# A hybrid decoder layer: T4 weight parts issued earlier in the mix stage, differences inside the attentions moved to VectorE, w_out's scaling spread

## The chip, the core and the metric

The kernel runs on one NeuronCore of a Trainium2 chip. The metric is the device time of one execution in microseconds (us). The engines are TensorE (PE, matmuls; PEld its weight loads), VectorE (DVE), ScalarE (ACT), GpSimd (POOL) and SyncE (SP), whose queue issues most of the transfers. TensorE writes its products to PSUM banks, ScalarE and VectorE read them there, GpSimd works on SBUF alone.

## What is computed

One layer with 2048 rows and a width of 1024, cut to its core:

```python
shift, scale, gate = split(silu(c) @ w_ada + b_ada)
u = x * (1 + scale) + shift
q, k, v, a_gate, p_in, p_gate, m_a, m_p = split(u @ w_in)
a = (sliding_window_sink_attention(q, k, v, sinks, bias) * silu(a_gate)) @ w_attn_proj
p = (group_linear(causal_pool(p_in)) * pool_scale * silu(p_gate)) @ w_pool_proj
y = ((sigmoid(m_a) * a + sigmoid(m_p) * p) @ w_out) * (1 + gate)
x = layer_norm(2 ** 0.25 * x + y) * ln_gain + ln_bias
```

All of it is in float32. Sixteen query heads share two heads of keys and values; the window is 128 rows.

## The kernel before

**Products by seven instead of eight.** Each large product is a Strassen-like scheme over 2 x 2 blocks. A weight block pair (a `Quad`) meets an input stored as seven sets, named B11, T1, T2, B21, T3, B22, T4: some are blocks of the input, some are differences of blocks. A product is made of 12 matmuls (`product`, line 314), because every float32 operand is split into a high and a low part: high times high (4 matmuls), high times low (4), low times high (4). The first eight need only the weights' high part, the last four the low part. The high part is a cast on ScalarE, the low part a subtraction on VectorE (`low`, line 131): `pair_split` (line 301) does two blocks at once, 128 x 1024, and `half_split` (line 307) one block, 128 x 512, for T4. Both write to `w_set` tiles, a ring of four buffers (line 167); a pair takes two, a half takes one.

**Rings.** Outside the attentions, `ring` (line 460) runs groups of two quads ("tiles"). For each group `back` (line 338) gives T2 and B21 of both tiles, then T3 and B22 of both, then T4 of both; `front` (line 328) then opens the next group with B11 and T1 of both. That is 14 products a group. T2, T3 and T4 of one tile add up in one bank `lg`; between T3 and T4 the sum `p5 = c + p5` (line 387) reads that bank. Each product is followed by `tick()`, which runs hooks: the loads, splits of sets, differences and stores that other stages hang into this group at a given position. `defer` puts work off by so many ticks, `q.consume` takes a finished result.

**Order.** Operations given through `act`, `dve`, `pool`, `pe` and `sp` (class `Ordered`, line 51) are pinned behind what was given out before them on their engine. Those given through `nc.scalar` and `nc.vector`, as in `back`, `pair_split` and `half_split`, can be moved by the framework's scheduler when they are ready sooner. Each engine then works its queue in order.

**Stages.** First ring (gates, keys, values, queries of the first half of the rows), attention of the first half, second ring, attention of the second half, then the mix stage: one leftover group, attention projection and pool projection of each half (two groups each, four phases), and the product with w_out. Only the quads of the four projection phases have gates to fetch (`ahead`). In the last group of a phase the hooks also split the sets of the next phase: `PLAN` and `SPLIT_AT` (lines 497 to 502) put them at ticks 2 to 7 and 11 to 13 of it, the rest into the next phase's first group. A set's half costs a ScalarE cast and a VectorE subtraction of 128 x 1024.

**Attentions.** `attention` (line 771) walks 64 blocks `n` of softmax work (scores, exponentials, transposes, values) and fills TensorE's time between them with products from `filling()`. `later(n, f)` runs `f` at the end of block `n`. All operations are pinned here. `sums_between` (line 996) hangs in, three times (at 39, 56 and 61), the differences T1, T2, T4 and T3 of the attention output that the mix stage will read: `sums_to` (line 199) loads two rooms of SBUF, makes four differences on GpSimd and stores them.

**w_out.** In the second ring, `second_phase` (line 1474) multiplies w_out by `cb` (1 + gate) on VectorE, row by row, before the same differences are made: the list `side`, hung in at the starts on line 1500; the last four starts are w_out's. In the first ring, `sums_to` does the same with x, modulated on ScalarE.

Of the kernel before, what the change touches and what calls it, by code (L numbers as in the profile page):

```python
# [60 lines left out]
def kernel(  # L61
# [134 lines left out]
    def put(q, store, name, i, src):  # L196
        q.dma_start(store[name][i // 2, :, i % 2, :], src)

    def sums_to(ph, store, i, load, work=None):

        b = []

        def x(r, c):
            return b[r][:, c * CH : (c + 1) * CH]

        def fetch():
            b.extend((ph.spare(), ph.spare()))
            b.reverse()
            for r in (1, 0):
                load(b[r], r)  # L210

        def sub(out, a, c):
            return lambda: pool.tensor_tensor(x(*out), x(*a), x(*c), ALU.subtract)

        todo = [(0, fetch)]
        if work:
            todo += [(4, lambda: work(b[0], 0)), (4.5, lambda: work(b[1], 1))]
        made = [("B11", (0, 0)), ("B21", (1, 0)), ("B22", (1, 1))] if work else []
        puts = [(5 + 0.6 * n, *x) for n, x in enumerate(made)]
        at = 7.5 if work else 4  # L220
        for out, a, c, name in (
            ((0, 1), (0, 1), (0, 0), "T1"),
            ((1, 1), (1, 1), (0, 1), "T2"),
            ((1, 0), (1, 0), (1, 1), "T4"),
            ((0, 0), (1, 1), (0, 0), "T3"),
        ):
            todo.append((at, sub(out, a, c)))
            puts.append((at + 2.5, name, out))
            at += 1.5
        for at, name, z in puts:  # L230
            todo.append((at, lambda name=name, z=z: put(sp, store, name, i, x(*z))))
        return sorted(todo, key=lambda t: t[0])
# [105 lines left out]
    def back(ph, grp, opened, nxt, own, tick):  # L338
        st = []
        for q in grp:  # L340
            if q.ahead:
                q.ahead(ph, 0)
                defer(2, lambda q=q: q.ahead(ph, 1))
        for q, (a, b, c, w, *copy) in zip(grp, opened):
            p5 = None if copy else ph.p("p5")
            if w is None:
                c = bank("lg")
                nc.scalar.copy(c, a)
                nc.scalar.copy(p5, b)
                w = pair_split(ph, q.second())[::-1]  # L350
                q.late()
                product(c, w[1], "T2")
            elif copy:
                p5 = copy[0]
            else:
                u2 = ph.p("u2")
                nc.scalar.copy(u2, a)
                if c is None:
                    c = bank("lg")
                    product(c, w[1], "T2", True)  # L360
                nc.vector.tensor_tensor(c, c, u2, ALU.add)
                nc.scalar.copy(p5, b)
            tick()
            if len(copy) < 2:
                nc.vector.tensor_tensor(b, c, p5, ALU.add)
            if not copy:
                product(a, w[0], "B21")
            tick()
            q.consume(ph, 0, 0, a)
            st.append((q, b, c, p5))  # L370
        w = {}

        def ask(q):

            defer(1, lambda: q.load(ph, own, nc.sync, None))
            defer(3, lambda: q.sum1(nc.gpsimd))

        def third(x):
            w[x] = opened[x][5] if len(opened[x]) > 5 else pair_split(ph, st[x][0].third())[::-1]
            if x < len(nxt):  # L380
                ask(nxt[x])

        def with_t3(x):
            q, b, c, p5 = st[x]
            product(c, w[x][1], "T3")
            tick()
            nc.vector.tensor_tensor(p5, c, p5, ALU.add)
            q.consume(ph, 1, 1, p5)

        def with_b22(x):  # L390
            q, b, c, p5 = st[x]
            product(b, w[x][0], "B22")
            tick()
            q.consume(ph, 0, 1, b)

        for x in range(len(st)):
            third(x)
            with_t3(x)
            with_b22(x)
        for q in nxt[len(st) :]:  # L400
            ask(q)
        for q, b, c, p5 in st:
            w = half_split(ph, q.a22)
            product(c, w, "T4")
            tick()
            q.consume(ph, 1, 0, c)

# [363 lines left out]
    def attention(ph, s, fills, post, opened):  # L771
# [18 lines left out]
        def later(n, f):  # L790
            coming.append((max(n, now_n[0]), len(coming), f))
# [202 lines left out]
            split(j)  # L994

        def sums_between(n0, i):
            for offset, f in [(0, rooms), *sums_to(ph, ain_d[s], i, load_raw(ain_d[s], i))]:
                later(n0 + int(offset / 2), f)

        def rooms():  # L1000
            ph.turns["spare"] = iter([kvp.tile([P, D], F32, tag=f"qs0{t}", name=f"room{t}") for t in range(2)])

        for i, n0 in enumerate((39, 56, 61)):
            sums_between(n0, i)
        fill = filling()
        lgs, exps, Ls, pvs, outs, ags = {}, {}, {}, {}, {}, {}
# [467 lines left out]
    def second_phase(ph, opened, post, plan1):  # L1474
        groups, fills, _, turn = plan1
        cb = ph.t.tile([P, D], F32, tag="cb", bufs=1, name="cb")
        hooks = {}

        def gate_rows():
            nc.scalar.dma_start(gate_d.rearrange("k p -> p k"), mod[:, 16:24], allow_slow_non_contiguous=True)  # L1480
            nc.scalar.dma_start(cb, gate_d.rearrange("k p -> (k p)").partition_broadcast(P))

        def load_wo(x, k):
            for n in range(2):
                sp.dma_start(cols(x, n), wout[k, n])

        side = []
        for raw, i in ((ain_d[0], 3), *((pin_d[0], i) for i in range(4))):
            side.append(sums_to(ph, raw, i, load_raw(raw, i)))
        for i in range(4):  # L1490
            ks = (i, 4 + i)
            side.append(sums_to(
                ph,
                wo_d,
                i,
                lambda x, r, ks=ks: load_wo(x, ks[r]),
                lambda x, r: dve.tensor_tensor(x, x, cb, ALU.mult),
            ))
        ahead, hooks = hooks, {}
        for start, todo in zip((14, 18, 22, 26, 30, 34, 39, 44, 50), side):  # L1500
            for offset, f in todo:
                at = int(start + offset) - 14
                hooks.setdefault((at // 14, at % 14), []).append(f)
        later_hooks, hooks = hooks, ahead
        hooks.setdefault((0, 2), []).append(gate_rows)
        planned(hooks, ph, u1_d, True)
        opened = ring(ph, [post], opened, hooks, groups[0], lambda tick: [front(ph, q, tick) for q in groups[0]])
        hooks = later_hooks
        planned(hooks, ph, None, False)
        hooks.setdefault((2, 0), []).append(lambda: ph.turns.clear())  # L1510
        turned(hooks, lambda i: turn(ph, i), 4)
        opened_by = [q for _, _, q in fills[:2]]
        return ring(ph, groups, opened, hooks, opened_by, lambda tick: [front(ph, opened_by[0], tick)])
# [147 lines left out]
```

## Time and profile before

| | |
|---|---|
| median of 3 runs | 1691.07 us (1689.7 to 1692.35) |
| profiled execution | 1694.21 us, its span 1692.1 us |
| granted TensorE clock | 0.997 |
| busy: PE, DVE, ACT, POOL | 1645.3, 1190.4, 1024.3, 968.4 us |
| first ring, first attention | 0 to 254, 254 to 600 us |
| second ring, second attention | 600 to 830, 830 to 1177 us |
| mix stage, with w_out from 1529 | 1177 to 1692 us |

In a line of the timeline stand start, duration, engine, source line, operation, output and input tiles, shapes and count; in brackets the idle time before it and what ended it. A line of waits gives engine, source line and tile, who was waited for, the total, how often, and the longest. L57 is the helper through which all pinned operations go, so groups are told apart by tiles. Of a merged line of matmuls the modelled end runs a little into the next line; starts are the better measure.

### The profile page before, as it was taken

The numbers are of one execution on the slowest core, as the hardware profiler recorded it, in microseconds if no ns is written. First come the engines' busy times: TensorE is split into PE (matmuls) and PEld (weight loads), VectorE is DVE, ScalarE is ACT, GpSimd is POOL, SyncE is SP. The second block draws the span as 40 slices with busy tenths as digits, with TensorE's granted clock in tenths as the row PEclk, the third lists the DMA queues.
The fourth block names the chain that finished last, engine by engine and source line by source line (L and its number), as shares of the span: only waits on it lengthen the run. The fifth ranks groups of instructions, "written<-read, shape, count | busy, mean of one in ns | idle before, by whom it ended". The sixth has DMA issues, their size and how long they took to land.

```text
span 1692.1 us, 24664 instructions
## 1 busy us (share of the span) xinstructions
PE 1645.3 (97%) x8058; PEld 1383.4 (82%) x8058; DVE 1190.4 (70%) x2132; ACT 1024.3 (61%) x2146; POOL 968.4 (57%) x734
## 2 busy tenths in 40 slices
PE   7999999999999999999999999999999999999997
PEld 6788888888888788878888888887877878787886
DVE  6845656677767666486567677675768896978777
ACT  4754547877777655335578777776746454544452
POOL 3333437685867948764476768598444463323442
PEclk9999999999999999999999999999999999999999
DMA  9688844333442688872533345345957885676443
GB/s 360 218 281 301 206 152 139 97 123 115 159 148 69 223 280 295 290 260 101 167 112 107 111 127 179 106 148 186 357 201 272 290 307 193 238 276 232 150 150 112
DMA packets 185969, 331.55 MB, mean 196 GB/s; under 512 B 18016, under 2 KB 43760, under 8 KB 185840
## 3 DMA queue, kind: packets, MB, share of 16 engines
q1 hardware_dynamic: 182720, 325.72, 56.3%
q10 hardware_dynamic: 3088, 4.23, 1.2%
q8 instruction: 64, 1.05, 0.2%
q14 instruction: 65, 0.53, 0.1%
q0 software_dynamic: 32, 0.02, 0.0%
HBM read 223.77 MB, written 109.28 MB: 197 GB/s over the span
## 4 chain that ended last, share of the span: by engine, by line
PE 76%; DVE 9%; ACT 5%; DMA 4%; issue 3%; POOL 2%; SPq 1%; POOLq 0%; DVEq 0%; ACTq 0%
PE mm L57 49%; PE lg L57 20%; PE pv L57 4%; PE pt L57 3%; DVE set_T L57 1%; DMA ma_d<-raw 1%; DVE w_set L132 1%; ACT L L57 1%; DMA g<-ma_d 1%; DVE w_set L57 1%; ACT w_set L57 1%; DVE g L624 1%; SPq L57 1%; DVE L L57 1%; DVE qs L57 1%
## 5 line engine op out<-in xcount | busy, mean ns | idle before, releaser
L57 PE MATMUL mm<-set_B,w_set 128*128 128x512 f32 x2664 | 653.2, 392 | 0.6 <-DVE w_set L57 0.5
L57 PEld LDWEIGHTS mm<-set_B,w_set 128*128 128x128 f32 x2664 | 496.6, 188 | 103.0 <-DVE w_set L57 0.9
L57 PE MATMUL mm<-set_T,w_set 128*128 128x512 f32 x1824 | 453.9, 395 | 8.1 <-DVE mm L57 6.0
L57 PE MATMUL lg<-set_T,w_set 128*128 128x512 f32 x1704 | 413.8, 392 | 14.3 <-DVE w_set L132 12.4
L57 PEld LDWEIGHTS mm<-set_T,w_set 128*128 128x128 f32 x1824 | 335.9, 188 | 77.8 <-DVE mm L57 11.5
L57 PEld LDWEIGHTS lg<-set_T,w_set 128*128 128x128 f32 x1704 | 319.9, 189 | 86.5 <-DVE w_set L132 16.3
L132 DVE TENSOR_TENSOR w_set<-W,w_set 128x1024 fp32r<-128x1024 f32 x137 | 193.5, 1413 | 141.8 <-ACT w_set L303 131.8
L303 ACT CAST w_set<-W 128x1024 fp32r<-128x1024 f32 x137 | 143.8, 1050 | 195.1 <-PE mm L57 146.0
L266 POOL TENSOR_TENSOR W<-W,A 128x512 f32<-128x512 f32 x46 | 74.3, 1615 | 273.9 <-DMA A<-in_win_dram 65.2
L57 POOL TENSOR_TENSOR w_set<-W,w_set 128x512 fp32r<-128x512 f32 x120 | 157.5, 1320 | 100.3 <-ACT w_set L57 93.7
L57 DVE TENSOR_TENSOR o<-pv,o 64x128 f32<-64x128 f32 x256 | 72.0, 281 | 134.9 <-ACT o L57 128.4
L57 POOL TENSOR_TENSOR W<-W 128x512 f32<-128x512 f32 x82 | 108.3, 1335 | 46.3 <-DVE sm L57 25.6
L57 ACT ACTIVATE L<-L,nm 128x257 f32<-128x257 f32 (+1 forms) x256 | 127.2, 499 | 12.4 <-DVE nm L57 3.6
L275 POOL TENSOR_TENSOR W<-W 128x512 f32<-128x512 f32 x46 | 72.1, 1566 | 103.3 <-DVE w_set L132 91.5
L57 DVE CUSTOM_DVE_ANT_0 L<-lg,bt,nsink 128x256 f32<-128x256 f32 (+1 forms) x256 | 111.6, 473 | 20.2 <-PE lg L57 7.1
L270 POOL TENSOR_TENSOR W<-W 128x512 f32<-128x512 f32 x44 | 75.3, 1714 | 78.1 <-DVE w_set L132 69.0
L57 ACT CAST w_set<-W 128x512 fp32r<-128x512 f32 (+1 forms) x165 | 101.8, 628 | 27.7 <-POOL W L57 16.7
L57 ACT COPY o<-pv 64x256 f32<-64x256 f32 x128 | 47.3, 369 | 78.6 <-PE pv L57 77.5
L271 POOL TENSOR_TENSOR W<-W 128x512 f32<-128x512 f32 x44 | 69.2, 1572 | 33.2 <-DMA W<-in_win_dram 20.3
L57 DVE TENSOR_TENSOR ptl<-pt,pth 128x512 fp32r<-128x512 f32 (+1 forms) x128 | 85.6, 669 | 1.3 <-ACT pth L57 1.0
L57 POOL TENSOR_TENSOR spare<-spare 128x512 f32<-128x512 f32 x48 | 77.6, 1623 | 11.6 <-ACT spare L57 5.7
L57 ACT ACTIVATE L<-L,sm 128x256 f32<-128x256 f32 (+1 forms) x128 | 64.3, 502 | 31.5 <-DVE sm L57 31.2
(233 smaller groups left out, 2419.0 us busy)
## 6 DMA issues: line engine op xcount, KB each, us to landing
W<-in_win_dram SPq DMA_DIRECT2D x42, 512.0 KB, 5.9
W<-in_win_dram SPq DMA_DIRECT2D x42, 256.0 KB, 4.1
A<-in_win_dram SPq DMA_DIRECT2D x42, 256.0 KB, 4.8
ag_d<-sig SPq DMA_DIRECT2D x32, 256.0 KB, 5.3
pg_d<-sig SPq DMA_DIRECT2D x32, 256.0 KB, 5.0
pg<-pg_d SPq DMA_DIRECT2D x32, 256.0 KB, 3.3
pin_B<-fin SPq DMA_DIRECT2D x32, 256.0 KB, 2.1
ag<-ag_d SPq DMA_DIRECT2D x32, 256.0 KB, 2.9
```

What stands on the lines that cost most here:

```text
L57: return lambda *args, **kw: self.tc.keep_in_program_order(op(*args, **kw))
L132: engine.tensor_tensor(dst, src, as32(hi), ALU.subtract)
L266: e.tensor_tensor(self.w[:, 1, :], self.w[:, 2, :], self.a22, ALU.add)
L270: e.tensor_tensor(x[:, 1, :], x[:, 1, :], x[:, 0, :], ALU.subtract)
L271: e.tensor_tensor(x[:, 2, :], x[:, 0, :], x[:, 2, :], ALU.subtract)
L275: e.tensor_tensor(x[:, 3, :], x[:, 3, :], x[:, 1, :], ALU.subtract)
L303: a.copy(by_two(hi), raw)
L624: nc.vector.tensor_tensor(g, src, g, ALU.mult)
```

## The change

Three things change.

1. In `back`, where the quads have gates (the four projection phases), the order in the text becomes: third split and T3 of the first tile, third split of the second tile, B22 of the first tile, the half splits for both T4 products, T3 and B22 of the second tile, both T4 products. The order of the products is the same. The load of the second successor, asked for in `third(1)`, moves with it. Without gates the order stays.
2. `sums_to` takes an engine. Inside the attentions it is VectorE; the steps of `sums_between` are rounded up instead of down, and the second of its three places is 55 instead of 56.
3. The second of two pieces of work on loaded rows (w_out's scaling, the modulation of x in the first ring) comes at step 5.5 instead of 4.5, and w_out's four rows start at 33, 36, 43 and 48 instead of 34, 39, 44 and 50.

```diff
-    def sums_to(ph, store, i, load, work=None):
+    def sums_to(ph, store, i, load, work=None, eng=pool):
...
-            return lambda: pool.tensor_tensor(x(*out), x(*a), x(*c), ALU.subtract)
+            return lambda: eng.tensor_tensor(x(*out), x(*a), x(*c), ALU.subtract)
...
-            todo += [(4, lambda: work(b[0], 0)), (4.5, lambda: work(b[1], 1))]
+            todo += [(4, lambda: work(b[0], 0)), (5.5, lambda: work(b[1], 1))]
...
-        for x in range(len(st)):
-            third(x)
-            with_t3(x)
-            with_b22(x)
-        for q in nxt[len(st) :]:
-            ask(q)
+        lasts = []
+        third(0)
+        with_t3(0)
+        if grp[0].ahead:
+            third(1)
+            with_b22(0)
+            lasts = [half_split(ph, q.a22) for q in grp]
+        else:
+            with_b22(0)
+            third(1)
+        with_t3(1)
+        with_b22(1)
         for q, b, c, p5 in st:
-            w = half_split(ph, q.a22)
-            product(c, w, "T4")
+            product(c, lasts.pop(0) if lasts else half_split(ph, q.a22), "T4")
             tick()
             q.consume(ph, 1, 0, c)
...
-            for offset, f in [(0, rooms), *sums_to(ph, ain_d[s], i, load_raw(ain_d[s], i))]:
-                later(n0 + int(offset / 2), f)
+            for offset, f in [(0, rooms), *sums_to(ph, ain_d[s], i, load_raw(ain_d[s], i), eng=dve)]:
+                later(n0 + math.ceil(offset / 2), f)
...
-        for i, n0 in enumerate((39, 56, 61)):
+        for i, n0 in enumerate((39, 55, 61)):
...
-        for start, todo in zip((14, 18, 22, 26, 30, 34, 39, 44, 50), side):
+        for start, todo in zip((14, 18, 22, 26, 30, 33, 36, 43, 48), side):
```

## The prediction

> **What bounds the kernel now.** I read first the page's table of busy times, then the list of TensorE's waits, then its timeline where the waits are long.
>
> ```profile
> span 1692.1 us, 24664 instructions
> PE 1645.3 (97%) x8058; PEld 1383.4 (82%) x8058; DVE 1190.4 (70%) x2132; ACT 1024.3 (61%) x2146; POOL 968.4 (57%) x734
> ```
>
> TensorE is busy nearly throughout, and the change neither adds nor removes a matmul. Only the gaps between matmuls can go. The waits of TensorE from 1258 to 1533 us, where the mix stage runs its attention and pool projections, are one row (total, times, longest):
>
> ```profile
> PE lg L57 <- DVE w_set L132: 10.1, 7, 2.8
> ```
>
> All seven are TensorE waiting for the low part of a split weight block, which `low` (line 132) makes on VectorE. Where they lie shows in TensorE's timeline. Four fences follow, one for the last group of each of these four phases: start, duration, operation, count, and in brackets the idle time and who ended it.
>
> ```profile
> 1274.94 2.88 PE L57 MATMUL lg<-set_T,w_set 128*128 128x512 f32 x12
> 1277.66 2.88 PE L57 MATMUL mm<-set_B,w_set 128*128 128x512 f32 x12
> 1280.38 1.98 PE L57 MATMUL lg<-set_T,w_set 128*128 128x512 f32 x8
> 1284.47 5.51 PE L57 MATMUL lg<-set_T,w_set 128*128 128x512 f32 x16 [2.11 <-DVE w_set L132]
> 1289.81 0.39 PE L57 MATMUL mm<-set_B,w_set 128*128 128x512 f32 x1
> ```
>
> ```profile
> 1360.53 1.98 PE L57 MATMUL lg<-set_T,w_set 128*128 128x512 f32 x8
> ...
> 1369.58 0.62 PE L57 MATMUL mm<-set_B,w_set 128*128 128x512 f32 x2
> ```
>
> ```profile
> 1440.31 1.98 PE L57 MATMUL lg<-set_T,w_set 128*128 128x512 f32 x8
> ...
> 1447.62 0.62 PE L57 MATMUL mm<-set_B,w_set 128*128 128x512 f32 x2
> ```
>
> ```profile
> 1518.37 1.98 PE L57 MATMUL lg<-set_T,w_set 128*128 128x512 f32 x8
> 1521.35 3.06 PE L57 MATMUL lg<-set_T,w_set 128*128 128x512 f32 x12 [1.01 <-DVE w_set L132]
> 1527.18 2.08 PE L57 MATMUL lg<-set_T,w_set 128*128 128x512 f32 x4 [2.77 <-DVE w_set L132]
> 1529.05 3.56 PE L57 MATMUL mm<-set_B,w_set 128*128 128x512 f32 x12
> ```
>
> The first fence begins with T3 and B22 of the second tile, unhindered; each then shows the first T4 product and ends with the first product of the next group (`front`). A product is 12 matmuls: eight with the weights' high part, four with the low part. In all four fences the first eight run and the low part is missing. An unhindered product takes 2.72 us from start to start (1274.94 to 1277.66), so two T4 products should take 5.44. They take 9.43, 9.05, 7.31 and 10.68, which is 3.99, 3.61, 1.87 and 5.24 too long. In the last, the next product's row is also 3.56 long where the clean product's is 2.88: 0.68 more. **Sum: 15.39 us.** Part of it is the clock: after the longest wait four matmuls take 1529.05 - 1527.18 = 1.87 us, 0.47 each, against 0.23.
>
> (The Trainium skill, "TensorE: Matmul & The Clock Gate", section "Why this matters for your kernels", puts the fall to half speed behind idle gaps of more than about 3 us. The trace differs: the 16 matmuls at 1284.47 lasted 5.51 us, so they too ran slowly, behind a wait of 2.11. By the rule the first group's loss would be the wait alone and a saving there about 1.9 us smaller; the rows decide.)
>
> **Why the parts are late.** VectorE's timeline in the first and the last of these groups:
>
> ```profile
> 1282.67 0.68 DVE L387 TENSOR_TENSOR p<-lg,p 128x512 f32<-128x512 f32 x1
> 1283.27 1.15 DVE L132 TENSOR_TENSOR w_set<-A,w_set 128x512 fp32r<-128x512 f32 x1
> ...
> 1287.28 1.21 DVE L132 TENSOR_TENSOR w_set<-W,w_set 128x1024 fp32r<-128x1024 f32 x1
> ...
> 1519.53 0.68 DVE L387 TENSOR_TENSOR p<-lg,p 128x512 f32<-128x512 f32 x1
> 1520.13 1.16 DVE L132 TENSOR_TENSOR w_set<-A,w_set 128x512 fp32r<-128x512 f32 x1
> 1521.22 1.77 DVE L624 TENSOR_TENSOR g<-p,g 128x512 f32<-128x512 f32 x1
> ...
> 1527.65 1.21 DVE L132 TENSOR_TENSOR w_set<-W,w_set 128x1024 fp32r<-128x1024 f32 x1
> ```
>
> L387 is the sum after T3 of the second tile, `w_set<-A` the low part for the first T4, `w_set<-W` the low part for the next group's first weights; operations of one shape last from 0.68 to 1.77 us here. ScalarE's high parts for both T4 products are ready long before:
>
> ```profile
> 1275.72 1.13 ACT L310 CAST w_set<-A 128x512 fp32r<-128x512 f32 x2
> ```
>
> So nothing but VectorE's queue holds the low part back: it stands behind the next phase's set splits and the sums of the second tile.
>
> **The change, part by part.**
>
> *Mix stage.* The parts for both T4 products are issued behind B22 of the first tile. Their buffers are those of the first tile's third pair, free when that B22 ends, at 1274.94 in the first group by TensorE's rhythm. The low parts come out early enough for T4 of the first tile: its wait goes. What is late next? First, the L387 sum: it reads the bank into which the second T4 accumulates, so that product cannot start before it. With the two low parts in front (1.15 and a clean 0.68), the sum that ended at 1283.35 ends at 1285.18. TensorE would want to start the second T4 at 1280.38 + 2.72 = 1283.10: a wait of 2.1 us is left. Second, the next group's low part: the queue ahead of it holds the same work, and VectorE has no idle in that stretch, so I leave it at 1287.28 + 1.21 = 1288.49. `front` then starts at 1283.10 + 2.72 + 2.08 = 1287.90 and needs the low part after eight matmuls, at 1289.7: no wait. Kept 2.1 of 3.99. In the last group: the sum ends at 1520.21 + 1.84 = 1522.05, wanted at 1521.09, wait 0.96; `front` at 1524.77 needs its part at 1526.58 and gets it at 1528.86, wait 2.28. Kept 3.24 of 5.92. Together 5.34 of 9.91 stays, 54%; I take the same share for the other two groups. **Gain 46% of 15.39 = 7.1 us**, with waits too short for the slow clock. Bounds: all of it (15.4), if the scheduler puts the sum and the next low part ahead; below nothing too, a few us, if the second tile's sums, pushed back by 1.8 us, hold up more than the second T4. The second tile's third split and the load of its successor's weights move up one product (2.7 us): both engines and SP's queue then issue the same instructions, TensorE's order is unchanged, and the load waits only for that split. I cost this at nothing: ScalarE's casts run at 1275.72 already, so behind them nothing on ScalarE comes later than now. Rings without gates keep their order.
>
> *Attention.* Twelve differences in each of two attentions move from GpSimd to VectorE:
>
> ```profile
> L57 POOL TENSOR_TENSOR room<-room x12: 1277/1292/1356, 473.7 to 1174.9; 128x512 f32<-128x512 f32 x12
> L57 POOL TENSOR_TENSOR room<-room,room x12: 1277/1298/2276, 475.1 to 1176.2; 128x512 f32<-128x512 f32 x12
> ```
>
> GpSimd is relieved of 1.3 us each time. Where that matters is the end of both attentions (the whole timeline, then TensorE's in the second):
>
> ```profile
> 566.96 1.28 POOL L57 TENSOR_TENSOR room<-room 128x512 f32<-128x512 f32 x1
> ...
> 574.81 0.62 ACT L57 CAST w_set<-W 128x512 fp32r<-128x512 f32 x1 [2.16 <-POOL W L57]
> ...
> 578.57 0.69 DVE L57 TENSOR_TENSOR mm<-mm,p 128x512 f32<-128x512 f32 x1
> ...
> 579.31 0.97 PE L57 MATMUL mm<-set_T,w_set 128*128 128x512 f32 x3 [2.08 <-DVE sm L57]
> ```
>
> ```profile
> 1156.55 0.96 PE L57 MATMUL mm<-set_T,w_set 128*128 128x512 f32 x3 [2.07 <-DVE mm L57]
> ```
>
> GpSimd makes two differences there (2.6 us) ahead of a weight sum for which ScalarE waits 2.16 us; ScalarE's softmax work, VectorE's and the sum `mm<-mm,p` follow in their queues, and TensorE waits 2.1 us for it. Without the differences the chain starts 2.2 us sooner and both waits go: 4.2 us. Against it stands VectorE's time. The trace of before has no such operation there. The rows of the first attention's groups (254 to 600 us; busy, mean ns, idle before and who ended it) give VectorE's idle in each block and a subtraction of the same shape:
>
> ```profile
> L57 DVE TENSOR_TENSOR o<-pv,o 64x128 f32<-64x128 f32 x126 | 35.4, 281 | 67.2 <-ACT o L57 64.0 <-POOL w_set L57 1.2 <-issue 0.5
> ...
> L57 DVE TENSOR_TENSOR w_set<-W,w_set 128x512 fp32r<-128x512 f32 x20 | 16.9, 843 | 5.3 <-ACT w_set L57 5.2
> ```
>
> A difference costs 0.84 us, 10 us an attention, with 0.68 and 1.77 as its ends. VectorE waits 64 us for ScalarE's copies in 63 blocks, 1.0 each: a difference issued at a block's end runs in that wait. Behind it stands the next block's softmax chain, and TensorE waits for that if the difference waits itself; but its data are loaded two blocks ahead. I put 0.4 us against it: **gain 3.8**; bounds 4.2 and a loss (the slower rival).
>
> *w_out's scaling.* Two multiplications in one step become one in each of two, and the later three rows start one to three steps earlier.
>
> ```profile
> 752.66 4.55 DVE L57 TENSOR_TENSOR spare<-spare,cb 128x1024 f32<-128x1024 f32 x2
> 757.14 3.56 DVE L132 TENSOR_TENSOR w_set<-W,w_set 128x1024 fp32r<-128x1024 f32 x2
> ```
>
> ```profile
> 759.50 1.21 PE L57 MATMUL lg<-set_T,w_set 128*128 128x512 f32 x4 [1.08 <-DVE w_set L132]
> ```
>
> The 4.55 us stand ahead of the split for which TensorE waits 1.1. They now stand earlier, but ahead of another split; I take **0.7**, bounds a loss of 1 and a gain of 1.4. The same spreading in the first ring touches only ScalarE, ahead of no wait: nothing.
>
> **Sum:** 7.1 + 3.8 + 0.7 = 11.6 us off. The profiled execution took 1694.21 us, 2.1 around its span and 3.1 above the median shown; the waits don't depend on that, so 1691.1 - 11.6 = **1679.5 us**.
>
> **Rivals.**
> 1. *All the T4 loss goes*: the scheduler, free to move what is not pinned, puts the second tile's sum and the next low part where TensorE wants them. For it: VectorE is busy 28.17 of 38 us over the first such group (the windows' row: length, PE, PEld, DVE, ACT, POOL, clock, DMA), so there is idle earlier.
>
> ```profile
> 1253.00:1291.00 38.00, 35.89 (x152) 29.25 (x151) 28.17 (x26) 21.45 (x28) 16.94 (x11) 0.96 0.87 306
> ```
>
> Against: none from 1282.67 to 1288. 15.4 + 3.8 + 0.7: 1671.
> 2. *The wait only moves*: VectorE's work up to `front` is the same, so the second T4 and `front` give most back, some 4 us gained in the mix stage; or the low parts, ready since 1276, don't come sooner because pinned set splits stay ahead. 4 + 2 to 3: 1685.
> 3. *Slower*: VectorE, not GpSimd, paces the attentions. A difference that meets GpSimd's own work lasts up to 1.77 us, and the softmax chain behind it is late by what the idle of 1.0 doesn't hide. If each of the 24 costs TensorE 0.84 it is 20.2 us against a gain of 7.1 + 4.2 + 0.7 = 12.0: 8 slower, 1699. It decides from 0.5 us each. Against it: the idle is as long as a mean difference. (The Trainium skill, "GPSIMD Engine Reference", section "Key points", says that GpSimd shares its SBUF interfaces with VectorE and contends with instructions with two SBUF inputs. The differences are such; the 1.77 against 0.68 is in line with it.)
> 4. *Nothing measurable*: the low parts are already placed by readiness, not by their place in the text, and the attentions give back their 4: 1689.
>
> **How the numbers follow.** Forecast (1675 to 1683) 0.45, rival 1 0.20, rival 2 0.18, rival 3 0.10, rival 4 0.07. The range that leaves out 2 in 10 goes from rival 1's 1670 to 1688, which takes in rival 2 and the bounds of VectorE's cost. Within 0.2% (3.4 us, about what a measurement of this kernel tells from no change) lies most of rival 4; faster 0.84, same 0.06, slower 0.10.
>
> **What would show it.** Right: no wait inside the first T4 product of the four groups; the low parts ahead of the L387 sum on VectorE; a short wait at the start of the second T4, and in the last group one at `front`; no wait near 579 and 1156 us; VectorE's differences at 0.7 to 1.2 us. Wrong: new waits of TensorE for `ptl` or `mm<-mm,p` between 460 and 600 us; the low parts still behind the sum; differences that wait for their loads.

## The result and the profile after

The changed kernel takes 1681.96 us (median of 6 runs, 1681.37 to 1682.15), the kernel before 1691.28 (6 runs beside it, 1689.7 to 1695.24). The ratio is 0.9941, interval 0.9929 to 0.9954: faster by 10 us (8 to 12). The profiled execution of the changed kernel took 1681.96 us, 1.8 around its span.

The page of the changed kernel, its span and busy times, and then rows of its list of TensorE's waits over the whole span (total, times, longest):

```profile
span 1680.2 us, 24662 instructions
...
PE 1644.0 (98%) x8058; PEld 1384.0 (82%) x8058; DVE 1205.3 (72%) x2156; ACT 1026.0 (61%) x2146; POOL 953.2 (57%) x710
```

```profile
PE mm L57 <- DVE mm L57: 3.6, 4, 1.5
...
PE pv L57 <- ACT pth L57: 2.2, 4, 1.1
PE lg L57 <- DVE p L387: 2.0, 1, 2.0
...
PE lg L57 <- DVE w_set L132: 0.6, 1, 0.6
```

The row for `w_set` of line 132, 10.1 us in the mix stage before, is 0.6 in the whole span. Two rows were not there in this size: 2.0 us behind the sum L387, and 2.2 behind ScalarE's `pth`, which is softmax work of the attentions.

TensorE's timeline in the last groups of phases 1, 2 and 4 of the changed kernel, from B22 of the second tile (`mm<-set_B`, or the last lines before `lg`) to the next group:

```profile
1274.70 2.88 PE L57 MATMUL mm<-set_B,w_set 128*128 128x512 f32 x12
1277.42 5.62 PE L57 MATMUL lg<-set_T,w_set 128*128 128x512 f32 x24
1282.88 2.88 PE L57 MATMUL mm<-set_B,w_set 128*128 128x512 f32 x12
```

```profile
1353.60 3.26 PE L57 MATMUL lg<-set_T,w_set 128*128 128x512 f32 x12
1358.09 2.98 PE L57 MATMUL lg<-set_T,w_set 128*128 128x512 f32 x12 [1.23 <-ACT w_set L303]
1360.91 1.98 PE L57 MATMUL mm<-set_B,w_set 128*128 128x512 f32 x8
1363.27 1.21 PE L57 MATMUL mm<-set_B,w_set 128*128 128x512 f32 x4 [0.39 <-DVE w_set L132]
1364.32 2.91 PE L57 MATMUL mm<-set_T,w_set 128*128 128x512 f32 x12
```

```profile
1508.51 2.88 PE L57 MATMUL lg<-set_T,w_set 128*128 128x512 f32 x12
1513.40 4.58 PE L57 MATMUL lg<-set_T,w_set 128*128 128x512 f32 x12 [2.01 <-DVE p L387]
1517.82 2.88 PE L57 MATMUL mm<-set_B,w_set 128*128 128x512 f32 x12
```

Measured as in the prediction, two T4 products from start to start against 5.44 us: phase 1 takes 1282.88 - 1277.42 = 5.46 and loses nothing (before: 3.99). Phase 2 loses 7.31 - 5.44 = 1.87, and `front` 0.69 more: 2.56 (before: 3.61). Phase 3 loses nothing (1.87). Phase 4 loses 9.31 - 5.44 = 3.87 (5.92): 2.17 as a wait and 1.70 in twelve slow matmuls behind it (1517.82 - 1513.40 = 4.42 against 2.72). **The T4 loss is 6.4 us instead of 15.4.** At 1358.09 the profile names ScalarE's cast, which had long run; what came last is again the sum L387 on VectorE, from 1357.27 to 1357.95. Of the 15.4 us before, 1.7 in phase 1 and 1.7 in phase 4 were matmuls at half the clock; of the 6.4 now, 1.7 in phase 4.

VectorE's timeline at these places, phase 1 first, then phase 4:

```profile
1274.69 1.77 DVE L132 TENSOR_TENSOR w_set<-A,w_set 128x512 fp32r<-128x512 f32 x1
1276.39 0.68 DVE L620 TENSOR_TENSOR wide<-mm,g 128x512 f32<-128x512 f32 x1
1276.99 1.19 DVE L132 TENSOR_TENSOR w_set<-A,w_set 128x512 fp32r<-128x512 f32 x1
1278.10 1.21 DVE L57 TENSOR_TENSOR set_T<-set_T 128x1024 fp32r<-128x1024 f32 x1
1279.23 0.68 DVE L387 TENSOR_TENSOR p<-lg,p 128x512 f32<-128x512 f32 x1
```

```profile
1508.03 3.48 DVE L132 TENSOR_TENSOR w_set<-A,w_set 128x512 fp32r<-128x512 f32 x2
1511.44 1.21 DVE L57 TENSOR_TENSOR set_T<-set_T 128x1024 fp32r<-128x1024 f32 x1
1512.57 0.68 DVE L387 TENSOR_TENSOR p<-lg,p 128x512 f32<-128x512 f32 x1
```

In phase 1 both low parts are done at 1278.18, and the sum at 1279.91, ahead of the second T4 at 1277.42 + 2.72 = 1280.14. In phase 4 the two low parts alone take 3.48 us (the prediction had put 1.84), a set split follows, and the sum ends at 1513.25, 2.0 late.

In the attentions the 24 differences now are VectorE's:

```profile
L57 DVE TENSOR_TENSOR room<-room x12: 678/1192/1783, 470.6 to 1171.7; 128x512 f32<-128x512 f32 x12
L57 DVE TENSOR_TENSOR room<-room,room x12: 679/686/1781, 476.8 to 1175.8; 128x512 f32<-128x512 f32 x12
```

They last 0.68 to 1.78 us. The wait of 2.08 at 579 is gone; of the 2.07 at 1156 there remains 0.43 at 1153.58. But there is a new one earlier (TensorE's timeline, first attention), and one of 0.31 and 0.62 at 1142 in the second:

```profile
566.90 0.50 PE L57 MATMUL pv<-pth,vv 128*128 128x256 f32 x2 [1.08 <-ACT pth L57]
568.03 0.80 PE L57 MATMUL pv<-ptl,vv 128*128 128x256 f32 x2 [0.62 <-DVE ptl L57]
```

Between the same two matmuls (starts 561.75 and 580.12 before, 561.47 and 579.76 now) the end of the first attention takes 18.37 us before and 18.29 now; that of the second (1139.62 to 1157.35 before, 1137.41 to 1154.38 now) takes 17.73 and 16.97. Both together gained 0.8 us. But behind the waits at 566.90 and 568.03 the matmuls now run at half the clock for 3.41 us, which costs 1.7, and in the trace of before none did so here: in waits alone 2.5 us went. In the second ring nothing is lost any more at 742 and 759 (0.43 and 1.38 us before).

### The profile page after: what moved, and what is told of

The parts are those of the page before. It is cut to its first block, busy times and chain, and to the rows that moved or that the text cites. A ratio compares the mean times of both kernels' runs of the same rounds, so it can differ in the third digit from the quotient of the medians.

```text
span 1680.2 us, 24662 instructions
## 1 busy us (share of the span) xinstructions
PE 1644.0 (98%) x8058; PEld 1384.0 (82%) x8058; DVE 1205.3 (72%) x2156; ACT 1026.0 (61%) x2146; POOL 953.2 (57%) x710
## 4 chain that ended last, share of the span: by engine, by line
PE 83%; DVE 7%; ACT 4%; POOL 2%; issue 2%; DMA 1%; SPq 0%; POOLq 0%; DVEq 0%; ACTq 0%
PE mm L57 52%; PE lg L57 23%; PE pv L57 4%; PE pt L57 3%; ACT L L57 1%; DVE w_set L132 1%; DVE set_T L57 1%; DVE w_set L57 1%; DVE L L57 1%; ACT w_set L57 1%; DVE qs L57 1%; POOL nxt L57 0%; POOL fin L57 0%; POOL w_set L57 0%; DVE g L629 0%
## 5 line engine op out<-in xcount | busy, mean ns | idle before, releaser
L57 POOL TENSOR_TENSOR w_set<-W,w_set 128x512 fp32r<-128x512 f32 x120 | 161.1, 1350 | 112.1 <-ACT w_set L57 110.2
L57 POOL TENSOR_TENSOR W<-W 128x512 f32<-128x512 f32 x82 | 109.7, 1352 | 53.0 <-DVE sm L57 25.9
L275 POOL TENSOR_TENSOR W<-W 128x512 f32<-128x512 f32 x46 | 72.8, 1583 | 107.1 <-DVE w_set L132 86.7
L270 POOL TENSOR_TENSOR W<-W 128x512 f32<-128x512 f32 x44 | 77.2, 1759 | 84.4 <-DVE w_set L132 71.0
L271 POOL TENSOR_TENSOR W<-W 128x512 f32<-128x512 f32 x44 | 72.6, 1650 | 29.5 <-DMA W<-in_win_dram 20.8
```

The source lines that it names most:

```text
L57: return lambda *args, **kw: self.tc.keep_in_program_order(op(*args, **kw))
L270: e.tensor_tensor(x[:, 1, :], x[:, 1, :], x[:, 0, :], ALU.subtract)
L271: e.tensor_tensor(x[:, 2, :], x[:, 0, :], x[:, 2, :], ALU.subtract)
L275: e.tensor_tensor(x[:, 3, :], x[:, 3, :], x[:, 1, :], ALU.subtract)
```

## The experiments

Each kernel ran five times or more, beside runs of the kernel before on the same chip; the medians of before were 1691.1 in the first four, 1691.9, 1691.2 and 1692.0 in the others. "T4 loss" is the sum over the four phases of what both T4 products and the products of `front` behind them take above 2.72 us each; "half clock" is the part of it in matmuls at half the clock. Both are of one profiled execution.

### The three parts alone

Only the new order in `back`, only the attentions' differences (with the rounding and the 55), only w_out's and x's spreading, each put into the kernel before; the diffs are those parts of the change. The fourth is the changed kernel with the load of the second successor asked for behind B22 of the first tile again:

```diff
-            if x < len(nxt):
+            if x < len(nxt) and not (x and grp[0].ahead):
                 ask(nxt[x])
...
             with_b22(0)
+            if len(nxt) > 1:
+                ask(nxt[1])
             lasts = [half_split(ph, q.a22) for q in grp]
```

> Before with the new order in back alone. Theory (VectorE's queue order held the low parts, and the earlier load keeps GpSimd out of VectorE's way): the four last groups lose about 6.5 us in place of 15.4, so 8 to 9 us off, some 1682.5. Rival (much of the gain comes from the attentions and w_out's scaling): 4 to 6 us off.

> Before with the attentions' differences on VectorE, their rounding and place 55 alone. Theory (GpSimd's relief is eaten because VectorE's differences take 1.77 us beside GpSimd and slow GpSimd's sums too): 0 to 1.5 us off. Rival (the prediction's: the relief counts in full): 3.8 us off.

> Before with the spread scaling and its earlier starts alone. Theory (the two waits of the second ring at 742 and 759 us go): 1.7 us off. Rival (the waits move to another split): 0.

> After, with the load of the second successor asked for behind B22 of the first tile again, everything else as in after. Theory (the earlier load lets GpSimd make its two weight sums before the late part of VectorE's queue, so that set splits there take 1.2 instead of 2.3 us): waits of 1 to 2 us come back at the second T4 of the first and third of the four phases, 2 to 4 us slower than after, some 1685. Rival (the order on VectorE is all there is to it): as after, 1682.

| kernel | median us | ratio to before | interval | T4 loss, us | half clock |
|---|---|---|---|---|---|
| new order in `back` alone | 1685.73 | 0.9963 | 0.9951 to 0.9975 | 6.9 | 1.7 |
| attentions alone | 1689.19 | 0.9987 | 0.9977 to 0.9996 | 10.4 | 0 |
| spreading alone | 1690.28 | 0.9993 | 0.9983 to 1.0002 | 11.8 | 1.7 |
| changed kernel, load late | 1682.61 | 0.9946 | 0.9933 to 0.9959 | 6.9 | 1.7 |

The parts add up: 0.37% + 0.13% + 0.07% = 0.57%, against 0.59% for the whole. In us, of 1691: 6.3 (4.2 to 8.3), 2.2 (0.7 to 3.9) and 1.2 (none to 2.9). The third part by itself is not told from no change by its time; its waits at 742 and 759 are gone, though. The load's place does nothing: my theory for that run has fallen.

The traces say the same where executions with the same code in a stage are averaged, between the same matmuls. The first attention takes 347.1 us with the differences on GpSimd (mean of three traces) and 345.9 with the change (seven), the second 346.8 and 346.0: 2.1 us gained. A single pair misleads: the three of the old code lie between 346.1 and 347.6 in the first attention, the trace of before being the shortest.

The last columns show something else. The second and third kernels have the old order in `back`, like the kernel before, and lose 10.4 and 11.8 us at T4, not 15.4. About half of the difference or more is the clock: the trace of before has 3.4 us of half clock here, the other two none and 1.7. Another part goes with a load. ScalarE's timeline at the start of phase 1's last group, in the kernel before, with the spreading alone and with the attentions alone:

```profile
1265.52 2.00 ACT L604 ACTIVATE g<-g 128x512 f32<-128x512 f32 x3 [1.06 <-DMA g<-ma_d]
```

```profile
1264.80 1.95 ACT L604 ACTIVATE g<-g 128x512 f32<-128x512 f32 x3 [0.45 <-DMA g<-ma_d]
```

```profile
1264.88 1.93 ACT L604 ACTIVATE g<-g 128x512 f32<-128x512 f32 x3
```

The gates' load lands 1.06 us, 0.45 us and not at all too late for ScalarE; its casts behind it come as much later, and so does VectorE's queue, which waits for them. Phase 1 loses 3.99, 1.99 and 0.93 us at T4 in these three, 1.7 of the 3.99 in slow matmuls. So the old order's loss differs from one execution to the next, with the clock and, in phase 1, with the landing of a load; this is read from the traces and wasn't tried by itself. The new order's loss is 6.4 to 6.9 in the three kernels so far that have it, with 1.7 of half clock in each.

### Is it the sum L387 that is left over?

Three edits of the changed kernel: the half splits one product later, so that the sum goes ahead of both low parts; the third split of the second tile back behind B22 of the first; the low parts for T4 on GpSimd.

```diff
-            lasts = [half_split(ph, q.a22) for q in grp]
...
         with_t3(1)
+        if grp[0].ahead:
+            lasts = [half_split(ph, q.a22) for q in grp]
```

> The changed kernel with the half splits for both T4 products given out one product later, behind T3 of the second tile, so that the sum L387 of that tile is issued ahead of both low parts. Theory (the sum behind the two low parts is what is left of the T4 loss): the waits in front of the second T4, 1.5 us at 1358 and 2.2 plus 1.7 of slow clock at 1513, shrink to under 0.5 each, the first T4 stays without a wait because its low part still comes before it, and the time falls by 3 to 5 us from 1682 to 1677 to 1679. Rival (VectorE has a fixed amount of work before the next group's first weights, so only the place of the wait moves): the loss of phases 2 and 4 stays at 5 to 7 us in sum, now inside the first T4 or at the front product, and the time is 1681 to 1684.

1683.78 us, ratio 0.9951 (0.9939 to 0.9964). TensorE in phases 2 and 4:

```profile
1357.76 3.94 PE L57 MATMUL lg<-set_T,w_set 128*128 128x512 f32 x16 [1.70 <-DVE w_set L132]
...
1364.24 1.20 PE L57 MATMUL mm<-set_B,w_set 128*128 128x512 f32 x4 [0.73 <-DVE w_set L132]
```

```profile
1513.15 3.96 PE L57 MATMUL lg<-set_T,w_set 128*128 128x512 f32 x16 [1.74 <-DVE w_set L132]
...
1519.63 1.20 PE L57 MATMUL mm<-set_B,w_set 128*128 128x512 f32 x4 [0.70 <-DVE w_set L132]
```

The rival holds. In phases 2 and 4 the sum is on time, and the wait sits inside the first T4 (16 matmuls left: the last four of that product and the second), as in the kernel before. T4 loss 6.7 instead of 6.4, and none of it is half clock: in waits it is 6.7 against 4.7. Which of the two stands first chooses the place of the wait; with the sum first the waits are no smaller.

```diff
-            third(1)
             with_b22(0)
+            third(1)
             lasts = [half_split(ph, q.a22) for q in grp]
```

> The changed kernel with the third split of the second tile (and the load of its successor) put back behind B22 of the first tile, still ahead of the half splits. Theory (the earlier third split, whose 128x1024 low part then runs in an idle stretch of VectorE, is what empties phases 1 and 3, which the prediction costed at nothing): waits of 1 to 2 us come back in each of phases 1 and 3, at T3 of the second tile or at the second T4, the T4 losses rise from 6.4 to 9 to 11 us, and the time is 1685 to 1687, no better than mix stage undone. Rival (the place of the two half splits does all of it): T4 losses stay at 6 to 7 us and the time at 1681.5 to 1683.

1685.11 us, ratio 0.9962 (0.9949 to 0.9976). Losses come back in phases 1 and 3, but small: 0.40 in the one, 0.58 in the other; the whole T4 loss is 6.9. VectorE's timeline in phase 1 shows the idle that the earlier third split used:

```profile
1270.04 1.23 DVE L57 TENSOR_TENSOR set_B<-set_B 128x1024 fp32r<-128x1024 f32 x1 [1.91 <-ACT set_B L57]
```

So the earlier third split is worth about 1.0 us in phases 1 and 3, not all of it, as my theory had it. In phase 4 this execution lost 0.5 less, but only because its wait of 2.47 us, longer than the 2.01 of the changed kernel, was followed by no matmuls at half the clock: in waits the T4 loss is 6.9 against 4.7. The time fits the theory, and the T4 loss as a whole the rival. Of the 3.2 us against the changed kernel the span of the profiled execution shows 1.4, and 1.0 us lies in the two attentions, which the edit doesn't touch. The rest stays open.

```diff
-    def half_split(ph, raw):
+    def half_split(ph, raw, d=nc.vector):
...
-        low(nc.vector, lo, raw, hi)
+        low(d, lo, raw, hi)
...
-            lasts = [half_split(ph, q.a22) for q in grp]
+            lasts = [half_split(ph, q.a22, nc.gpsimd) for q in grp]
```

> The changed kernel with the two low parts for T4 made on GpSimd instead of VectorE, in the four projection phases and the groups before them. Theory (VectorE's load in these stretches is what is left over): with 2.4 us less of it in each group the waits before the second T4 and at the front product go, and the time falls by 2 to 5 us to 1677 to 1680. Rival (GpSimd's queue with the weight sums of the next groups stands ahead of the low parts, and each meets VectorE's own work): the low parts take 1.5 to 2.3 us and come later than the first T4 wants them, waits of 2 us and more in all four phases, 1685 to 1695.

1681.01 us, ratio 0.994 (0.9928 to 0.9953). GpSimd's and then TensorE's timeline in phase 4:

```profile
1508.57 3.44 POOL L132 TENSOR_TENSOR w_set<-A,w_set 128x512 fp32r<-128x512 f32 x2
```

```profile
1515.54 3.00 PE L57 MATMUL lg<-set_T,w_set 128*128 128x512 f32 x12 [1.56 <-DVE p L387]
```

Neither holds. The T4 loss falls to 4.0 (2.1 in phase 2, 1.9 in phase 4), but 1.7 of the fall is half clock that this execution didn't meet; in waits it falls from 4.7 to 4.0, and the median by 1. The sum L387 still comes 1.56 late in phase 4, behind a set split that takes 2.31 us on VectorE (1.21 in the changed kernel). So taking the low parts off VectorE removes little of the rest. Elsewhere this execution lost 4.0 us instead of 1.5 at T3 at 1230, where ScalarE's sigmoids wait for the gates' load (2.4 us in its list of waits, 1.1 in the changed kernel). A later kernel with its low parts on VectorE lost 4.1 there too, so that isn't this edit; 1.7 us of each is half clock.

### What the differences cost in the attentions

Without the four of the second place; the second and third places moved from 55 and 61 to 58 and 64; the second place back on GpSimd:

```diff
         def sub(out, a, c):
+            if eng is None:
+                return lambda: None
...
-load_raw(ain_d[s], i), eng=dve)]:
+load_raw(ain_d[s], i), eng=None if i == 1 else dve)]:
```

> The changed kernel without the four differences of the second of the three places (blocks 55 to 60) in each attention; their rooms are loaded and stored undifferenced, so these parts of what the mix stage reads are left without the subtraction. It bounds what these eight differences cost where they now stand. Theory (VectorE's differences beside GpSimd's weight sums at blocks 57 to 60 slow both and make the waits at 567 and 1142): the waits of 2.1 and 0.7 at 567 to 571 and 1.3 and 0.7 at 1142 to 1154 shrink by half or more, and the time falls by 2 to 4 us to 1678 to 1680. Rival (those waits come from the softmax chain and GpSimd's weight sums as such): waits and time stay, 1681 to 1683.

```diff
-        for i, n0 in enumerate((39, 55, 61)):
+        for i, n0 in enumerate((39, 58, 64)):
```

> The changed kernel with the second and third places of the differences at blocks 58 and 64 instead of 55 and 61, so that the four of the second place run at the ends of blocks 60 to 63, when GpSimd's stretch without idle (530 to 577 us) is nearly over. Theory (these differences cost 3.3 us, the gain of leaving them out, because they run beside GpSimd's pool and weight sums and slow both): the waits at 567 to 571 and at 1142 fall from 2.8 and 1.3 to about 1.2 and 0.6, as without the differences, and the time to 1679 to 1680.5. Rival (VectorE has no room for them in any of these blocks): the waits only move to blocks 60 to 64 or to the first products of the next ring, time 1681 to 1684.

```diff
-load_raw(ain_d[s], i), eng=dve)]:
+load_raw(ain_d[s], i), eng=pool if i == 1 else dve)]:
```

> The changed kernel with the differences of the second place alone back on GpSimd, at the changed places. Theory (there they stand in GpSimd's queue ahead of the weight sum that ScalarE waits for, as before): the waits of 2.1 to 2.4 at 579 and 1156 come back, those at 567 and 1142 shrink to 1.1 and 0.6, and the time is 1682 to 1684. Rival (what these differences cost is their share of a busy stretch, whichever engine makes them): same sum of waits and the time within 1 us of the changed kernel's 1682.

| kernel | median us | interval of the ratio to before | us at the ends of the two attentions |
|---|---|---|---|
| changed | 1681.96 | 0.9929 to 0.9954 | 18.3, 17.0 |
| without the second place | 1678.66 | 0.9914 to 0.9938 | 16.1, 15.4 |
| second place later | 1679.64 | 0.9926 to 0.9951 | 17.2, 15.9 |
| second place on GpSimd | 1685.88 | 0.996 to 0.9982 | 18.4, 18.2 |

The last column is the time between the same matmuls as above (18.4 and 17.7 before). The theories hold for the waits, but for a new one of 0.49 at 574 with the second place later, and the time with it on GpSimd lies above its 1682 to 1684. On GpSimd the old waits are back (TensorE's timeline):

```profile
579.33 0.96 PE L57 MATMUL mm<-set_T,w_set 128*128 128x512 f32 x3 [2.08 <-DVE sm L57]
```

```profile
1154.75 1.46 PE L57 MATMUL mm<-set_T,w_set 128*128 128x512 f32 x3 [2.06 <-DVE mm L57]
```

That kernel's profiled execution also lost 4.1 us at 1232, so its time overstates them. On VectorE the eight differences (two attentions) cost 3.3 us by the medians where the change put them, and 3.5 over both whole attentions in the two traces, 1.7 of it in the half clock at 568, which the kernel without them doesn't meet. Running behind GpSimd's busy stretch (the third place moved with them) they cost 2.3 less by the medians. Measured against before on the same chip, the ratios of that kernel and of the changed one (0.9939 and 0.9941) can't be told apart; the traces show 1.5 us less over both whole attentions. How they cost it shows on GpSimd, in the kernel before and the changed one:

```profile
558.10 1.06 POOL L57 TENSOR_TENSOR nxt<-vb 128x526 f32<-128x526 f32 x1
559.24 2.19 POOL L57 TENSOR_TENSOR nxt<-nxt 128x524 f32<-128x524 f32 x2
561.51 1.29 POOL L57 TENSOR_TENSOR fin<-nxt 128x512 f32<-128x512 f32 x1
```

```profile
557.84 1.51 POOL L57 TENSOR_TENSOR nxt<-vb 128x526 f32<-128x526 f32 x1
559.43 2.72 POOL L57 TENSOR_TENSOR nxt<-nxt 128x524 f32<-128x524 f32 x2
562.23 1.30 POOL L57 TENSOR_TENSOR fin<-nxt 128x512 f32<-128x512 f32 x1
```

The same pool sums begin 0.26 us sooner and end 0.73 later, beside VectorE's work of these blocks, the difference at 556.65 (1.78 us) and what it pushes back. The first three additions take 0.98 us longer; TensorE's new wait at 566.90 is 1.08. With the second place later they take 1.06 and 2.19 again, and the difference runs at its clean 0.68 (that kernel's VectorE):

```profile
574.28 0.68 DVE L57 TENSOR_TENSOR room<-room 128x512 f32<-128x512 f32 x1
```

GpSimd is busy nearly throughout here. Two rows of the changed kernel's windows (stretch, its length, busy PE, PEld, DVE, ACT, POOL, then clock, DMA share and GB/s):

```profile
545.00:560.00 15.00, 15.00 (x85) 13.02 (x84) 11.49 (x31) 9.65 (x29) 14.69 (x13) 1.00 0.47 159
560.00:575.00 15.00, 13.30 (x65) 11.23 (x64) 12.12 (x24) 10.34 (x29) 14.77 (x12) 0.89 0.64 219
```

And ScalarE waits for GpSimd's weight sum (its timeline in the changed kernel; `pth` is what TensorE waits for at 566.90):

```profile
564.81 0.63 ACT L57 CAST w_set<-W 128x512 fp32r<-128x512 f32 x1 [3.36 <-POOL W L57]
...
566.27 0.58 ACT L57 CAST pth<-pt 128x512 fp32r<-128x512 f32 x1
```

### What stands ahead of the sum, and both gains together

```diff
-    SPLIT_AT = (2, 3, 4, 5, 6, 7, 11, 12, 13, 14, 15, 16, 17, 18)
+    SPLIT_AT = (2, 3, 4, 5, 8, 9, 11, 12, 13, 14, 15, 16, 17, 18)
```

> The changed kernel with the two set splits of T2 in the last group of a phase hung in at ticks 8 and 9 instead of 6 and 7, so that none of them stands on VectorE between the low parts for T4 and the sum L387. Theory (the sum is late in phases 2 and 4 for what is pinned ahead of it): the sum comes 1.2 to 2.3 us sooner, the waits in front of the second T4 (1.5, and 2.2 with 1.7 of slow clock) go to under 0.7 each, and the time falls by 2 to 4 us to 1678 to 1680. Rival (the sum of VectorE's work up to the next group's low parts is what counts): the splits delay the low part for the front product, waits of 1.5 to 3 us there in phases 2 and 4, time 1681 to 1684.

1680.75 us, ratio 0.9945 (0.9931 to 0.9958), which is not told from the changed kernel's 0.9941. TensorE in phases 2 and 4:

```profile
1367.75 1.19 PE L57 MATMUL mm<-set_B,w_set 128*128 128x512 f32 x4 [1.60 <-DVE w_set L132]
```

```profile
1511.34 3.00 PE L57 MATMUL lg<-set_T,w_set 128*128 128x512 f32 x12 [0.93 <-DVE p L387]
```

Each is right for one phase. In phase 4 the wait falls from 2.01 to 0.93 and the slow matmuls go; in phase 2 it moves to the third product of `front`. T4 loss 3.7 instead of 6.4, in waits 3.7 instead of 4.7; its median gains 1.2.

The last kernel has this and the later places in the attentions together:

> Both of the last two edits that helped in one kernel: second and third places of the differences at 58 and 64, T2's set splits at ticks 8 and 9. If the two are independent (different stages), the gains add: 1.8 to 2.3 us in the attentions and 1.2 to 2.9 in the mix stage off the changed kernel's 1682, so 1677 to 1679, with waits at 567 to 574 of 2 us in sum, none at 1154, and T4 losses of 3.4. Rival (VectorE's load is shifted from one to the other, or the medians of the two runs were chance): 1680 to 1682, with a wait of 2 us or more back in one of these places.

**1678.51 us** (1677.66 to 1679.48), ratio 0.992 (0.9906 to 0.9934): 3.5 us below the changed kernel, whose fastest run was 1681.37. By the medians the gains add up (2.3 and 1.2); the intervals of this ratio and the changed kernel's just overlap. The ends of the attentions take 17.6 and 15.9 us, and the T4 loss is 3.9, all in phases 2 and 4 and none of it half clock.

## Why the prediction was right, and where its steps were off

**The sign and the three places** were right. Of 11.6 us forecast, 10 came (8 to 12), and the time, 1682.0, lies 2.5 above the forecast, inside its own range of 1675 to 1683.

**Mix stage: 7.1 forecast, 6.3 measured alone.** The step "its wait goes" for the first T4 held in phases 1, 3 and 4, and in phase 2 but for 0.4 us. "First, the L387 sum" was right as to what is late next in phases 2 and 4. Two terms in it were wrong, in opposite directions:

- *"the sum that ended at 1283.35 ends at 1285.18"*: I put both low parts right in front of the sum. They began 2 to 5 us ahead of it, as ScalarE's high parts allowed, and phases 1 and 3 lost nothing where 2.1 and 1.0 were to stay. I had costed the earlier third split at nothing; it filled an idle of 1.9 us on VectorE and is worth 0.4 to 0.6 us in each of them. In phase 4 the same sum erred the other way: the two low parts took 3.48 us where I had put 1.84.
- *"with waits too short for the slow clock"*: in the last phase I divided the rest into 0.96 before the second T4 and 2.28 at `front`. It all came before the second T4, and 2.01 us of waiting cost 1.70 more in slow matmuls.

What is kept was thus 6.4 us, forecast 8.3, and in the profiled executions the stage gained 9.0. That isn't what the medians gained, since *"the waits don't depend on that"* failed: I took the 15.4 us of one execution for the typical one. It had taken 1694.21, near the top of the runs; the same order lost 10.4 and 11.8 us in two other kernels. Between the same matmuls its whole mix stage took 3.5 and 3.6 us longer than theirs, about the 3.1 by which it lay above the median. So its excess most likely stood in the very losses from which I worked out the gain. That 7.1 came near 6.3 is luck in part: the loss was taken too large, and the share of it that goes too small (46%; 15.4 to 6.4 is 58%).

**Attentions: 3.8 forecast, 2.2 measured alone.** The interval of that, 0.7 to 3.9, still holds the forecast; that it was too high rests on the traces (2.1 on average). "Both waits go" was right: 579 empty, 1156 down to 0.43. The step that failed is *"I put 0.4 us against it"*. I looked for the price in VectorE's idle, and its softmax chain mostly had that room. The price was paid on GpSimd: the engine that the edit relieves is the one that an operation on VectorE, placed beside its pool sums, slows from 1.06 to 1.51 us. In the first attention the half clock came on top. (The Trainium skill, "GPSIMD Engine Reference", section "Key points", says that the two engines share interfaces to SBUF; the prediction drew from it only that VectorE's 0.68 becomes 1.77. The rows show both sides paying.) Rival 3 named the contention, but its price, 0.84 for each of 24, was far too high: the eight differences of the second place cost 3.3 us in sum by the medians, 0.4 each.

**w_out: 0.7 forecast, 1.2 measured alone** (none to 2.9). Both waits went; here the forecast lies inside the interval.

**Rivals.** Rival 1 came true in phases 1 and 3, in part for the reason that it gave, idle earlier. Rival 2 is what phases 2 and 4 do, as the sum put first and, in phase 2, the splits put later show: there VectorE's work is nearly fixed up to `front`, and order mostly chooses the place of the wait. The times of rivals 3 and 4, 1699 and 1689, are excluded by the interval.

## What to carry to other kernels

Before waits are added up to a gain, ask how the profiled execution lies among the runs: one that is 3 us above the median may hold these 3 us in the very waits that are to go. Count the slow matmuls apart from the waits, too: whether a wait brings them differs from one execution to the next, and they hid here that two edits had lengthened the waits. An operation moved off a saturated engine still costs that engine time where it runs beside it; look for a stretch in which the other engine is idle, not only for idle time on the new one. Where one engine's work up to a deadline is fixed, reordering moves the wait, and only taking work away or past the deadline shortens it.

## What the runs showed of the hardware

- The clock falls for one fixed stretch at a time. It is granted at 0.50 for 3.41 us and then at 1.00 again, and these stretches lie on one grid: between the two in the kernel before lie 238.9 us, 70 times 3.413. What counts is how long TensorE idles within one stretch of the grid, not how long a wait is. Rows of the windows (length, busy PE and so on, clock, DMA share, GB/s), first of the kernel before, then of the one with the third split late:

```profile
1281.28:1284.69 3.41, 1.30 (x6) 0.79 (x5) 3.41 (x4) 0.28 (x1) 1.74 (x2) 1.00 1.03 390
1284.69:1288.10 3.41, 3.41 (x9) 2.66 (x9) 3.41 (x5) 2.41 (x3) 0.00 (x0) 0.50 1.06 397
1288.10:1291.51 3.41, 3.41 (x16) 2.82 (x16) 3.41 (x5) 1.30 (x2) 1.28 (x1) 1.00 1.05 387
```

```profile
1511.55:1514.96 3.41, 1.72 (x8) 1.10 (x6) 3.41 (x3) 1.04 (x1) 2.28 (x2) 1.00 1.03 402
1514.96:1518.37 3.41, 2.63 (x12) 2.19 (x13) 3.41 (x7) 1.06 (x1) 0.00 (x0) 1.00 0.45 174
```

The 2.11 us of idle time in the first row are followed by half the clock. The wait of 2.47 in the second kernel is split over two stretches, 1.69 and 0.78, and is not. In the fourteen traces (their starts and ends aside) a stretch with more than 1.93 us idle was always followed by one at half the clock, one with less than 1.67 never; between them both occur, and the ends of matmuls are modelled, so these bounds are rough. A stretch at half the clock costs 1.7 us. This also fits the runs without a profile: those of the kernel before took 1694.0 us on average where the granted clock was 0.994, and 1689.8 where it was 0.998.
- The price of a two-input VectorE operation beside GpSimd is paid on both: 0.68 becomes 1.78 us for 128x512, and GpSimd's 1.06 becomes 1.51 for 128x526.
- A load that lands about 1 us later, with `back` the same, went with a loss of 4.0 us in phase 1 instead of 0.9, by way of ScalarE's queue, VectorE's queue and then the clock. Behind the same kind of load the group from 1215 to 1253 us lost 0.7 to 4.1 us from one trace to another, 1.7 of the 4.1 in half clock; nothing tried here removes that.
